# Forgetting attention on one core: one row of 24 score matmuls per head pair, the value products behind it, and two steps issued in another order

## The chip, the cores and the metric

The kernel runs on one core of one Trainium2 chip. The time is the device time of one execution in microseconds (us); three executions were timed, and one more was profiled.

## The reference

A decoder trunk of two layers works on a stream of 512 rows and 1024 columns. The first layer has dilated sliding-window attention and a convolutional feed-forward part; the second, which this case is about, has forgetting attention (16 heads of 64) and a feed-forward part of the same kind. Keys, values and the cumulative log of the forget gates `c` are shared and computed once.

```python
def fox_mixer(xn, w_q, w_o, k, v, c):
    q = (xn @ w_q).reshape(B, T, B_HEADS, HEAD_DIM)
    c_t = c.transpose(0, 2, 1)
    for i in range(T // BLK):                  # four blocks of 128 queries
        q0, q1 = i * BLK, (i + 1) * BLK
        s = jnp.einsum('bqhd,bkhd->bhqk', q[:, q0:q1], k[:, :q1]).astype(jnp.float32) * scale
        s = s + (c_t[:, :, q0:q1, None] - c_t[:, :, None, :q1])
        s = jnp.where(causal, s, NEG)
        p = jax.nn.softmax(s, axis=-1).astype(v.dtype)
        outs.append(jnp.einsum('bhqk,bkhd->bqhd', p, v[:, :q1]))
    o = jnp.concatenate(outs, axis=1)
    return o.reshape(B, T, B_WIDTH) @ w_o
```

## The kernel before

The instructions of every engine are issued in the order in which the program names them. Each engine takes its own in that order and waits where an operand or a buffer is not ready. Products of full precision are made from a high and a low half of each operand, with three matmuls (`mm3`).

The attention stage is a loop over 32 units and three more steps (line 1708). A unit is (j, i): head pair j of 0 to 7, query block i of 0 to 3. A unit passes through several steps, each in a later round of the loop:

- `f_scores` (line 1619): TensorE multiplies queries and keys, 12 matmuls for two blocks of a pair, with two heads side by side in the two 64-row halves of the array. Blocks 0 and 1 share two PSUM banks; blocks 2 and 3 take two banks each. It is called at i = 0 and at i = 2.
- `f_bias` (line 1607): GpSimd makes the forget bias and the causal mask, one unit ahead.
- `f_exp` (line 1633): VectorE adds the bias to the scores and takes the row's maximum in one instruction for each head; ScalarE takes the exponential and its sum.
- `f_norm` (line 1646): VectorE divides the last unit's probabilities by their sums ("scaling").
- `f_transpose` (line 1656): two rounds behind, TensorE turns the probabilities over into PSUM, 2, 4, 6 or 8 blocks of 128 x 128 for i = 0 to 3, and ScalarE copies them out.
- `f_pv` (line 1672): TensorE multiplies them with the values ("value products", 40 matmuls for a pair with a 64-column form of the array). This is done for a whole pair at once, when the loop is at block 2 of the next pair, behind that round's transposes. `f_out_high` (ScalarE) and `f_out_low` (VectorE) then split the output in two halves.

Between these rows TensorE works on the queries of pairs ahead: `q_part(j, i)` (line 1537) is a quarter, six matmuls of 512 columns; `q_high` (ScalarE) and `q_low` (VectorE) split the sum. In the last pairs there are no queries left, and one group of six output-projection matmuls (`po.both`, tile `acc`) a round takes their place.

Weights come in pieces of 512 KB. `W.high` (ScalarE) makes the high half. The low half is made by `W.low` on VectorE (pairs 0, 1 and from 6 on), or, in pairs 2 to 5, by `W.minus` (ScalarE writes the negative of the high half) and `W.low_added` (a DMA issued on GpSimd adds the raw piece). Eight PSUM banks and pools of SBUF buffers are shared; raw pieces, gate rows, biases and probabilities take their buffers from one pool of ten (`p4`).

The lines that set the order of scores, scaling and products:

```python
            if i % 2 == 0:
                f_scores(j, (i, i + 1))
        if 1 <= n <= N:
            f_norm(*units[n - 1])
        if live:
            f_exp(j, i)
        ...
        if n % 4 == 2 or n == N:
            while pv_next < n - 2:
```

Of the kernel before, what the change touches and what calls it, by code (L numbers as in the profile page):

```python
# [117 lines left out]
def trunk_kernel(ctx, tc, x, norm_gains, w_qkv_a, w_o_a, w_q_b, w_o_b, kv_norm, w_kvf, b_f,  # L118
# [11 lines left out]
    def t8(shape, dt=F32, name="t8"):  # L130
        return p8.tile(shape, dt, tag="t8", name=name)

    def t4(shape, dt=F32, name="t4"):
        return p4.tile(shape, dt, tag="t4", name=name)

    def t2(shape, dt=F32, name="t2"):
        return p2.tile(shape, dt, tag="t2", name=name)

    def bank(shape, name="bank"):
        return psp.tile(shape, F32, tag="ps", name=name)  # L140

    def small(n, name):
        return sml.tile([128, n], F32, tag=name, name=name)
# [73 lines left out]
    W = Weights(nc, new_raw, lambda: t8([128, 2, 1024], F32R, name="w"), pieces)  # L217
# [64 lines left out]
    def mm3(o, ah, al, bh, bl, first, last, shared=False):  # L282
        pe.matmul(o, ah, bh, start=first, stop=False, skip_group_check=shared)  # L283
        pe.matmul(o, ah, bl, start=False, stop=False, skip_group_check=shared)  # L284
        pe.matmul(o, al, bh, start=False, stop=last, skip_group_check=shared)  # L285
# [78 lines left out]
    def xs(xT, kc, s):  # L364
        return xT[0][kc // 4][:, kc % 4, s], xT[1][kc // 4][:, kc % 4, s]
# [205 lines left out]
    def down_sums(pairs, place, queue, lag, behind):  # L571


        live, n = [], len(pairs)
        for i in range(n + lag + behind):
            if i < n:
                l, j = pairs[i]
                a, b = place()
                live.append((a, b))
                r = w_down[l][j * 256:j * 256 + 256, :].rearrange("(c p) d -> c p d", p=128)  # L580
                sp.dma_start(a, r[0])
                sp.dma_start(b[:, 0:512], r[1, :, 512:1024])
                sp.dma_start(b[:, 512:1024], r[1, :, 0:512])
            if 0 <= i - lag < n:
                a, b = live[i - lag]
                dve.tensor_tensor(a[:, 0:512], a[:, 512:1024], a[:, 0:512], ALU.subtract)
                dve.tensor_tensor(a[:, 512:1024], b[:, 0:512], a[:, 512:1024], ALU.subtract)
                dve.tensor_tensor(b[:, 0:512], b[:, 0:512], a[:, 0:512], ALU.subtract)
                dve.tensor_tensor(b[:, 512:1024], b[:, 512:1024], b[:, 0:512], ALU.subtract)
            i -= lag + behind  # L590
            if i >= 0:
                l, j = pairs[i]
                for q, t in enumerate(live[i]):
                    queue.dma_start(dT[l][j, :, q * 1024:q * 1024 + 1024], t)
            yield
# [932 lines left out]
    def load_ck(j):  # L1528
        t = t4([128, 2, T], name="ck")
        s = cd[2 * j:2 * j + 2, :]  # L1530
        sp.dma_start(t, bass.AP(tensor=s.tensor, offset=s.offset, ap=[[0, 128], [T, 2], [1, T]]))
        cks[j] = t
# [4 lines left out]
    def q_part(j, i):  # L1537

        if j >= 8:
            return  # L1540
        if i == 0:
            qps[j] = (bank([128, T], name="q_ps"), [t.rearrange("p (k c) -> p k c", k=8) for t in W.get()])
        o, (wh, wl) = qps[j]
        for kc in (2 * i, 2 * i + 1):
            bh, bl = xs(xTq, kc, ALL)
            mm3(o, wh[:, kc, :], wl[:, kc, :], bh, bl, kc == 0, kc == KD - 1)
# [72 lines left out]
    def f_scores(j, blocks):  # L1619
        wide = blocks[0] >= 2  # L1620
        if not wide:
            both = [bank([128, 2, 256], name="s_ps") for _ in range(2)]
        k = kst[j // 2][:, j % 2]
        for i in blocks:
            nn = max(256, (i + 1) * 128)
            sc[j, i] = [bank([128, T], name="s_ps") for _ in range(2)] if wide else [o[:, i] for o in both]
            for qp, kp in ((0, 0), (0, 1), (1, 0)):
                for hh in range(2):
                    own = slice(64 * hh, 64 * hh + 64)
                    pe.matmul(sc[j, i][hh][:, :nn], qT[j][own, qp, i * 128:(i + 1) * 128], k[own, kp, :nn],  # L1630
                              start=qp + kp == 0, stop=qp == 1)

    def f_exp(j, i):
        n = (i + 1) * 128
        s = sc.pop((j, i))
        bias = bia.pop((j, i))
        p = t4([128, 2, T], name="prob")
        nm, ls = small(2, "nm"), small(2, "ls")
        for hh in range(2):
            dve.tensor_tensor_reduce(p[:, hh, :n], s[hh][:, :n], bias[:, hh, :n], -0.125, BIG, ALU.add, ALU.min,  # L1640
                                     nm[:, hh:hh + 1])
            act.activation(p[:, hh, :n], p[:, hh, :n], AF.Exp, bias=nm[:, hh:hh + 1], scale=-1.0,
                           accum_out=ls[:, hh:hh + 1])
        prob[j, i] = (p, ls)

    def f_norm(j, i):
        n = (i + 1) * 128
        p, ls = prob[j, i]
        rl = small(2, "rl")
        dve.reciprocal(rl, ls)  # L1650
        for hh in range(2):
            dve.tensor_scalar(p[:, hh, :n], p[:, hh, :n], rl[:, hh:hh + 1], None, ALU.mult)
# [3 lines left out]
    def f_transpose(j, i):  # L1656
        p, _ = prob.pop((j, i))
        for hh in range(2):
            if i >= 2 or hh == 0:
                o = bank([128, 4, 128], name="pT_ps")  # L1660
                t = t2([128, 4, 128], name="pT")
            k0 = (i + 1) * hh if i < 2 else 0
            for k in range(i + 1):
                pe.transpose(o[:, k0 + k, :], p[:, hh, k * 128:(k + 1) * 128], ident)
            if i >= 2 or hh == 1:
                act.copy(t[:, :k0 + i + 1], o[:, :k0 + i + 1])
            pT[j, i, hh] = t[:, k0:k0 + i + 1]
# [4 lines left out]
    def f_pv(j, i):  # L1672
        if i == 0:
            ops[j] = bank([128, T], name="o_ps")
        o = ops[j]
        for k in range(i + 1):
            for hh in range(2):
                hd = 2 * j + hh
                pe.matmul(o[64 * hh:64 * hh + 64, i * 128:(i + 1) * 128],
                          Vt[hd // 8][:, k, (hd % 8) * 64:(hd % 8) * 64 + 64], pT[j, i, hh][:, k, :],  # L1680
                          start=k == 0, stop=k == i)
        del pT[j, i, 0], pT[j, i, 1]

    def f_out_high(j):
        o = ops[j]
        if j % 2 == 0:
            OTb[j // 2] = t8([128, 2, 2, T], F32R, name=f"OTb{j // 2}")
        t = OTb[j // 2]
        act.copy(t[:, 0, j % 2, :], o)
# [5 lines left out]
    units = [(j, i) for j in range(8) for i in range(4)]  # L1695
# [9 lines left out]
    N = len(units)  # L1705
    pv_next = 0
    down1 = down_sums([(1, 9), (1, 10)], in_one, pool, 2, 0)
    for n in range(N + 3):
        live = n < N
        if live:  # L1710
            j, i = units[n]
            if i == 0 and j + 1 < 8:
                load_ck(j + 1)
            if i % 2 == 0:
                f_scores(j, (i, i + 1))
        if 1 <= n <= N:
            f_norm(*units[n - 1])
        if live:
            f_exp(j, i)
            if n + 1 < N:  # L1720
                f_bias(*units[n + 1])
            if i == 1:
                q_low(j + 1)
                if 2 <= j < 6:
                    W.minus()
                    W.low_added()
            if i == 2 and j < 2 or (j, i) >= (6, 2):
                W.low()
            if i == 3 and j:
                f_out_low(j - 1)  # L1730
            q_part(j + 1 + (i > 0), (i + 3) % 4)
            if (j, i) in ((7, 1), (7, 2)):
                next(down1)
        if 2 <= n < N + 2:
            f_transpose(*units[n - 2])
        if n >= N + 3 - len(fill):
            po.both(*fill[n - N - 3 + len(fill)])

        if n % 4 == 2 or n == N:
            while pv_next < n - 2:  # L1740
                ju, iu = units[pv_next]
                pv_next += 1
                f_pv(ju, iu)
                if iu == 3:
                    f_out_high(ju)
        if live and i == 0:
            q_high(j + 1)
        if live and (i == (j < 2) if j < 6 else (j, i) >= (6, 1) and W.n_split < wo + 4):
            W.high()
# [53 lines left out]
```

## Time and profile before

| | us |
|---|---|
| median of 3 runs | 1109.83 (1109.48 to 1110.65) |
| profiled execution | 1109.52 |
| its span, first to last instruction | 1107.7 |
| TensorE busy | 1098.7 |
| VectorE busy | 876.4 |
| ScalarE busy | 674.2 |
| GpSimd busy | 210.0 |

The span is 1.8 us shorter than the time of the same execution. In the timelines each row has the start and the duration in us, the engine (PE is TensorE's matmuls, PEld its weight loads, DVE VectorE, ACT ScalarE, POOL GpSimd, SP SyncE), the line of the kernel, the operation, the tile written and the tiles read, shapes, and how many such instructions follow one another. In brackets stands how long the engine was idle before it and what ended that. Matmuls overlap, so the distance from start to start tells more than the duration.

### The profile page before, as it was taken

The numbers are of one execution on the slowest core, as the hardware profiler recorded it, in microseconds if no ns is written. First come the engines' busy times: TensorE is split into PE (matmuls) and PEld (weight loads), VectorE is DVE, ScalarE is ACT, GpSimd is POOL, SyncE is SP. The second block draws the span as 40 slices with busy tenths as digits, with TensorE's granted clock in tenths as the row PEclk, the third lists the DMA queues.
The fourth block names the chain that finished last, engine by engine and source line by source line (L and its number), as shares of the span: only waits on it lengthen the run. The fifth ranks groups of instructions, "written<-read, shape, count | busy, mean of one in ns | idle before, by whom it ended". The sixth has DMA issues, their size and how long they took to land.

```text
span 1107.7 us, 18081 instructions
## 1 busy us (share of the span) xinstructions
PE 1098.7 (99%) x6609; PEld 951.8 (86%) x6609; DVE 876.4 (79%) x1493; ACT 674.2 (61%) x1116; POOL 210.0 (19%) x309
## 2 busy tenths in 40 slices
PE   9999999999999999999999999999999999999997
PEld 6988889899999988888888788789999999988886
DVE  6697788888778689997685676868887788779894
ACT  7654565755666656576451587746656666747572
POOL 2532001311111211000001445400411111211000
PEclk9999999999999999999999999999999999999999
DMA  9799854467887979793448435594368878989862
GB/s 324 171 381 412 310 161 134 98 181 190 207 199 185 245 263 328 268 333 103 152 134 301 156 96 127 163 285 121 84 178 208 197 186 189 231 266 324 314 247 76
DMA packets 184928, 236.26 MB, mean 213 GB/s; under 512 B 12352, under 2 KB 132152, under 8 KB 184840
## 3 DMA queue, kind: packets, MB, share of 16 engines
q1 hardware_dynamic: 169224, 182.94, 51.0%
q0 software_dynamic: 14944, 52.18, 20.7%
q8 instruction: 52, 0.85, 0.3%
q14 instruction: 36, 0.29, 0.1%
q10 hardware_dynamic: 672, 0.00, 0.0%
HBM read 166.08 MB, written 39.63 MB: 186 GB/s over the span
## 4 chain that ended last, share of the span: by engine, by line
PE 96%; DVE 1%; ACT 1%; issue 1%; POOL 1%; DMA 0%; DVEq 0%; SPq 0%; POOLq 0%; ACTq 0%
PE up L284 13%; PE up L283 13%; PE up L285 13%; PE acc L283 8%; PE acc L284 8%; PE acc L285 8%; PE v_ps L283 2%; PE v_ps L285 2%; PE v_ps L284 2%; PE qk_ps L284 2%; PE qk_ps L283 2%; PE qk_ps L285 2%; PE q_ps L283 1%; PE first L285 1%; PE first L283 1%; PE first L284 1%
## 5 line engine op out<-in xcount | busy, mean ns | idle before, releaser
L283 PE MATMUL acc<-w 128*128 128x512 f32 (+1 forms) x311 | 120.6, 388 | 0.3 <-DVE mix L332 0.3
L285 PE MATMUL acc<-w 128*128 128x512 f32 (+1 forms) x311 | 120.4, 387 | 0.0
L284 PE MATMUL acc<-w 128*128 128x512 f32 (+1 forms) x267 | 103.2, 387 | 0.0
L78 DVE TENSOR_TENSOR w<-wraw,w 128x1024 fp32r<-128x1024 f32 x62 | 82.3, 1347 | 22.9 <-ACT w L60 22.5
L283 PE MATMUL up<-xsh,w 128*128 128x256 f32 x352 | 99.6, 283 | 0.0
L284 PE MATMUL up<-xsl,w 128*128 128x256 f32 x352 | 99.6, 283 | 0.0
L285 PE MATMUL up<-xsh,w 128*128 128x256 f32 x352 | 99.6, 283 | 0.0
L60 ACT CAST w<-wraw 128x1024 fp32r<-128x1024 f32 x82 | 84.7, 1051 | 18.7 <-PE v_ps L284 6.9
L620 ACT ACTIVATE bb<-up,conv 128x512 f32<-128x512 f32 x80 | 59.8, 778 | 58.3 <-DVE up L1007 47.6
L284 PE MATMUL up<-xcl,w 128*128 128x512 f32 (+1 forms) x276 | 93.5, 339 | 0.0
L284 PE MATMUL up<-xbl,w 128*128 128x512 f32 (+1 forms) x276 | 93.5, 339 | 0.0
L283 PE MATMUL up<-xbh,w 128*128 128x512 f32 (+1 forms) x276 | 93.5, 339 | 0.0
L283 PE MATMUL up<-xch,w 128*128 128x512 f32 (+1 forms) x276 | 93.5, 339 | 0.0
L285 PE MATMUL up<-xbh,w 128*128 128x512 f32 (+1 forms) x276 | 93.4, 338 | 0.0
L285 PE MATMUL up<-xch,w 128*128 128x512 f32 (+1 forms) x276 | 93.4, 338 | 0.0
L283 PEld LDWEIGHTS acc<-w 128*128 128x128 f32 x311 | 58.4, 188 | 12.6 <-DVE mix L332 0.7
L285 PEld LDWEIGHTS acc<-w 128*128 128x128 f32 x311 | 58.4, 188 | 11.9
L283 PEld LDWEIGHTS up<-xsh,w 128*128 128x128 f32 x352 | 67.6, 192 | 0.0
L284 PEld LDWEIGHTS up<-xsl,w 128*128 128x128 f32 x352 | 67.6, 192 | 0.0
L285 PEld LDWEIGHTS up<-xsh,w 128*128 128x128 f32 x352 | 67.6, 192 | 0.0
L621 DVE SCALAR_TENSOR_TENSOR bb<-up,conv,bb 128x511 f32<-128x511 f32 x80 | 59.5, 744 | 6.2 <-ACT bb L620 6.1
L623 DVE SCALAR_TENSOR_TENSOR bb<-up,conv,bb 128x510 f32<-128x510 f32 x80 | 59.9, 749 | 2.8
(312 smaller groups left out, 3151.8 us busy)
## 6 DMA issues: line engine op xcount, KB each, us to landing
wraw<-in_w_up_dram SPq DMA_DIRECT2D x88, 512.0 KB, 5.4
w<-wraw POOLq DMA_DIRECT2D x32, 512.0 KB, 6.4
dT<-dsums SPq DMA_DIRECT2D x28, 512.0 KB, 7.0
w<-wsum POOLq DMA_DIRECT2D x24, 512.0 KB, 5.7
dsums<-in_w_down_dram SPq DMA_DIRECT2D x22, 512.0 KB, 7.6
dsums<-in_w_down_dram SPq DMA_DIRECT2D x44, 256.0 KB, 7.8
hD<-hc POOLq DMA_DIRECT2D x44, 256.0 KB, 6.9
dact<-hD SPq DMA_DIRECT2D x44, 256.0 KB, 5.6
```

What stands on the lines that cost most here:

```text
L60: self.nc.scalar.copy(pair[:, 0], raw)
L78: self.nc.vector.tensor_tensor(pair[:, 1], raw, pair[:, 0].bitcast(F32), ALU.subtract)
L283: pe.matmul(o, ah, bh, start=first, stop=False, skip_group_check=shared)
L284: pe.matmul(o, ah, bl, start=False, stop=False, skip_group_check=shared)
L285: pe.matmul(o, al, bh, start=False, stop=last, skip_group_check=shared)
L620: act.activation(bb[:, s, :], ps, AF.Identity, bias=cp[:, 3, ch:ch + 1], scale=cp[:, 2, ch:ch + 1])
L621: dve.scalar_tensor_tensor(bb[:, s, 1:], ps[:, :T - 1], cp[:, 1, ch:ch + 1], bb[:, s, 1:], ALU.mult, ALU.add)
L623: dve.scalar_tensor_tensor(bb[:, s, 2:], ps[:, :T - 2], cp[:, 0, ch:ch + 1], bb[:, s, 2:], ALU.mult, ALU.add)
```

## The change

The scores of blocks 0 and 1 of the first pair are issued ahead of the loop. At block 2 of each pair the loop issues a query quarter, then the scores of this pair's blocks 2 and 3 and those of the next pair's blocks 0 and 1 as one row of 24, and then the value products of the pair before; the query quarter that this round had further back is left out there. Within a round the maxima and exponentials (`f_exp`) are issued ahead of the last unit's scaling (`f_norm`). `W.minus` and `W.low_added` move behind the round's transposes. In the last rounds the value products stay where they were.

```diff
+    outs = []
+
+    def values_of(n):
+        nonlocal pv_next
+        while pv_next < n - 2:
+            j, i = units[pv_next]
+            pv_next += 1
+            f_pv(j, i)
+            if i == 3:
+                outs.append(j)
+
+    f_scores(0, (0, 1))
     for n in range(N + 3):
         live = n < N
         if live:
             j, i = units[n]
             if i == 0 and j + 1 < 8:
                 load_ck(j + 1)
-            if i % 2 == 0:
-                f_scores(j, (i, i + 1))
+            if i == 2:
+                q_part(j + 2, 1)
+                f_scores(j, (2, 3))
+                if j + 1 < 8:
+                    f_scores(j + 1, (0, 1))
+                values_of(n)
+        if live:
+            f_exp(j, i)
         if 1 <= n <= N:
             f_norm(*units[n - 1])
         if live:
-            f_exp(j, i)
             if n + 1 < N:
                 f_bias(*units[n + 1])
             if i == 1:
                 q_low(j + 1)
-                if 2 <= j < 6:
-                    W.minus()
-                    W.low_added()
...
-            q_part(j + 1 + (i > 0), (i + 3) % 4)
+            if i != 2:
+                q_part(j + 1 + (i > 0), (i + 3) % 4)
...
             f_transpose(*units[n - 2])
+        if live and i == 1 and 2 <= j < 6:
+            W.minus()
+            W.low_added()
...
-        if n % 4 == 2 or n == N:
-            while pv_next < n - 2:
-                ju, iu = units[pv_next]
-                pv_next += 1
-                f_pv(ju, iu)
-                if iu == 3:
-                    f_out_high(ju)
+        if n >= N and n % 4 in (0, 2):
+            values_of(n)
+        while outs:
+            f_out_high(outs.pop())
```

## The prediction

> **What bounds the kernel now.** I read the page first, then the busy time of the attention stage by windows, then TensorE's timeline there, and last the timelines of the engines that feed it.
>
> ```profile
> PE 1098.7 (99%) x6609; PEld 951.8 (86%) x6609; DVE 876.4 (79%) x1493; ACT 674.2 (61%) x1116; POOL 210.0 (19%) x309
> ```
>
> TensorE is busy for 99% of the span, so only TensorE time counts, and its busy time also hides waits, because the ends of matmuls are modelled. The stage that the change touches runs from about 620 us, the first score matmul, to about 728 us. One head pair in the middle of it, by windows (columns: PE, PEld, DVE, ACT, POOL busy):
>
> ```profile
> 655.50:668.50 13.00, 13.00 (x110) 10.54 (x109) 8.58 (x30) 10.16 (x27) 6.95 (x13) 1.00 0.51 114
> ```
>
> TensorE fills the 13 us; VectorE has 4.4 us spare, ScalarE 2.8, and the granted clock is 1.00. TensorE's timeline of the same pair (start, us, operation), where the distance between starts is the cost:
>
> ```profile
> 655.96 0.98 PE L1630 MATMUL s_ps<-kst,qst 64*128 64x256 f32 x12
> 656.87 0.50 PE L283 MATMUL q_ps<-xqh,w 128*128 128x512 f32 x1
> ...
> 658.36 0.82 PE L1664 MATMUL pT_ps<-ident,prob 128*128 128x128 f32 x6
> 658.94 0.48 PE L283 MATMUL q_ps<-xqh,w 128*128 128x512 f32 x1
> ...
> 660.40 1.03 PE L1664 MATMUL pT_ps<-ident,prob 128*128 128x128 f32 x8
> 661.37 1.49 PE L1630 MATMUL s_ps<-kst,qst 64*128 64x384 f32 x12
> 662.78 0.50 PE L283 MATMUL q_ps<-xqh,w 128*128 128x512 f32 x1
> ...
> 664.28 0.38 PE L1664 MATMUL pT_ps<-ident,prob 128*128 128x128 f32 x2
> 664.59 2.40 PE L1679 MATMUL o_ps<-pT,Vt 128*64 128x128 f32 x40
> 666.92 0.50 PE L283 MATMUL q_ps<-xqh,w 128*128 128x512 f32 x1
> ...
> 668.95 0.98 PE L1630 MATMUL s_ps<-kst,qst 64*128 64x256 f32 x12
> ```
>
> A period is 668.95 - 655.96 = 12.99 us: two score rows of 0.91 and 1.41, four groups of six query matmuls, transposes in rows of 6, 8, 2 and 4, and 40 value products of 2.33. Nothing waits, but the price of a row depends on what follows it. Here are the other neighbours, and the places where TensorE does wait:
>
> ```profile
> 627.43 0.38 PE L1664 MATMUL pT_ps<-ident,prob 128*128 128x128 f32 x2
> 627.57 0.48 PE L283 MATMUL q_ps<-xqh,w 128*128 128x512 f32 x1
> ...
> 634.99 1.87 PE L1630 MATMUL s_ps<-kst,qst 64*128 64x384 f32 x12
> 636.79 0.50 PE L283 MATMUL q_ps<-xqh,w 128*128 128x512 f32 x1
> ...
> 703.08 0.66 PE L1664 MATMUL pT_ps<-ident,prob 128*128 128x128 f32 x4
> 703.49 0.48 PE L283 MATMUL acc<-w,OTb 128*128 128x512 f32 x1
> ...
> 708.62 1.17 PE L1664 MATMUL pT_ps<-ident,prob 128*128 128x128 f32 x8 [0.41 <-DVE prob L1652]
> ...
> 710.77 0.39 PE L285 MATMUL acc<-w,OTb 128*128 128x512 f32 x1
> 711.09 2.01 PE L1630 MATMUL s_ps<-kst,qst 64*128 64x384 f32 x12
> 713.39 0.44 PE L1664 MATMUL pT_ps<-ident,prob 128*128 128x128 f32 x2 [0.30 <-ACT pT L1666]
> ...
> 722.32 1.09 PE L1664 MATMUL pT_ps<-ident,prob 128*128 128x128 f32 x8
> 723.17 0.48 PE L283 MATMUL acc<-w,OTb 128*128 128x512 f32 x1
> ```
>
> Two transposes cost 0.14 ahead of query matmuls (627.43), but 0.31 ahead of value products (664.28). Eight cost 0.85 ahead of ordinary matmuls (722.32), but 0.97 ahead of scores (660.40). Four cost 0.41 even right behind value products (703.08). An ordinary matmul ahead of scores takes 0.32 (710.77) against the usual 0.23. Waits: the score row at 634.99 takes 1.80 where 661.37 takes 1.41, so 0.4 is lost; at 708.62 0.57 is lost (the last product ahead started 0.81 earlier and needs 0.23); at 711.09 the row takes 2.0 instead of 1.41 and 0.3 more follow. That is 0.4 in the first pair and 1.5 in the last two.
>
> **The change, part by part.**
>
> *Score rows of 24, value products behind.* Nothing is added or removed; rows are moved. Per pair TensorE now runs: six query matmuls ahead of scores (660.40 - 658.94 = 1.46, plus 0.09 for the switch, 1.55), 24 scores (1.41 + 0.91 = 2.32), a switch x, 40 products (2.33), two transposes ahead of query matmuls (0.14), six matmuls (1.46), four transposes (0.41), 1.46, six transposes (0.58), 1.46, eight transposes (0.85). The sum is 12.56 + x. The price x of going from scores straight to products is not in the trace. From below it is about 0, which is what two transposes ahead of query matmuls show; from above 0.17, the difference of 0.31 and 0.14 that products cost behind transposes. I take 0.08, in between, because both neighbours are array-form changes, and neither is nearer. A period is then 12.64, which saves 0.35.
>
> The Trainium skill, TensorEngine Tiling (Array Packing), Overview, says that a change of tiling mode drains TensorE. The 0.09 to 0.17 per switch above agree, and by that rule alone x would be a full switch at 0.17, a period 12.73, and the gain 0.6 us smaller over seven rows.
>
> The four periods between the first and fifth row of products save 4 x 0.35 = 1.4. In front of the first row of products the same terms save 0.4, and the 0.4 wait goes, because the second pair's query is split several rows ahead of its scores: 0.8.
>
> *What feeds the moved rows.* The scores of the next pair's blocks 0 and 1 now come two units earlier. Their query low half (q_low) is issued one unit ahead on VectorE. Counting a period from the query matmuls ahead of the score row, q_low ends at about 12.2 us and its scores start at 12.6 + 2.9 = 15.5: cover 3.3. Banks: 6 for scores, 1 for the query sum, 1 for the products make all 8; the last two come from the transposes of the pair before, copied by about 1.8, needed at 2.9 and 3.9: cover 1.1, which costs its lack if gone. The copy of (j,0) and the high half of the output (f_out_high) now stand behind the products on ScalarE, with exp(j,3) queued behind both:
>
> ```profile
> 667.04 0.59 ACT L1689 CAST OTb<-o_ps 128x512 fp32r<-128x512 f32 x1 [1.43 <-PE o_ps L1679]
> 667.52 0.73 ACT L1642 ACTIVATE prob<-prob,nm 128x512 f32<-128x512 f32 x1
> ```
>
> ScalarE already waits 1.43 there for the products, and exp(j,3) already stands behind that. Now: products end at 6.3, transposes 6.4, copy until 6.9, output 7.4 (0.48 from start to start, 667.04 to 667.52), exp of two heads 1.43 until 8.8, scaling of the first head 9.7. Its transposes are due at 12.64 - 0.85 = 11.8: cover 2.1. Cost nothing.
>
> *Minus of weight pieces later* (pairs 2 to 5). GpSimd's row behind the weight DMA, and the landing of that DMA in this stage (512 KB each, us) and in the whole kernel:
>
> ```profile
> 655.79 0.94 POOL L1612 TENSOR_SCALAR bias<-ck,cq 128x256 f32<-128x256 f32 x2 [1.28 <-DMA w<-wraw]
> ```
>
> ```profile
> w<-wraw POOLq DMA_DIRECT2D x4, 512.0 KB, 5.5
> ```
>
> ```profile
> w<-wraw POOLq DMA_DIRECT2D x32, 512.0 KB, 6.4
> ```
>
>  ScalarE copies the transposes of (j-1,3) first (two copies, 0.95), then does the minus. The products, now due earlier, gain that; the DMA that adds the piece is issued about 1 us later on GpSimd, and bias(j,3) is queued behind it. Minus ends at about 2.8, issue 0.7, bias 2.1: 5.6. The maximum of (j,3) then runs from 5.6 to 6.8, its exp was to start at 7.4 anyway. Cover 1.1; SyncE's queue is passed by nothing, and the query group that moves ahead of the scores issues no DMA (only a pair's first group takes a weight). The piece is used a pair later, so its 5.5 us landing is covered.
>
> *Maxima ahead of scaling.* VectorE's work is the same; exp starts earlier by one scaling (0.5 to 1.2), scaling later by one maximum (0.4 to 1.2), against 2 us of cover. Nothing in the middle of the stage.
>
> *The last two pairs.* Query matmuls are gone, output products fill in one group a unit. Rows: the 34.9 us from the fifth row of products to the end of the loop (692.9 to 727.8) include one score row of 0.91 that is now done earlier, so 34.0 stand against 32.0 of the new order without waits. Does it wait? VectorE's queue: the first late weight's high half ends on ScalarE at 699.9 (new time), then its low half 1.2, maximum (6,3) 1.2, scaling (6,2) 1.1, second low half 1.2, output low 0.6, maximum (7,0) 0.4, first head's scaling (6,3) 0.8: 706.5. TensorE reaches the transposes of (6,3) at 705.5. The low half is the longest of these terms on VectorE, a row of before:
>
> ```profile
> 702.19 1.23 DVE L78 TENSOR_TENSOR w<-wraw,w 128x1024 fp32r<-128x1024 f32 x1
> ```
>
> So one wait of 1.0 remains in place of 1.5, for 33.0: saved 1.0.
>
> Sum: 0.8 + 1.4 + 1.0 = 3.2, call it 3.1. Behind the stage TensorE waits for no engine for more than 0.4 us at once, so the gain is kept. The profiled execution took 1109.52, the median of the runs is 1109.83, 0.31 above it; against the profiled one the forecast is 1106.4, against the median 1106.7, the number that I give. x at 0 or 0.17 moves it by 0.6 either way, the last wait at 0 or 2 us by 1.0; both are seldom at one end, so I take 2.0 to 4.2 saved.
>
> **Rivals.**
>
> *The switches are worth little and the waits only move.* x is 0.17 and the last pairs lose 1.5 to 2 as before, since VectorE's queue there holds the same instructions. For it: 708.62 already waits for a scaling, and my own re-adding leaves 1.0. Saved: 0.4 + 0.4 + 4 x 0.26 + 0.3, less about 0.4 for longer waits: 1.7, to 1108.1. That is within 0.2% (2.2 us), about what a measurement of this kernel can tell from no change.
>
> *A buffer loop through the weight DMA makes it slower.* The pool of ten 4-KB-row buffers holds raw weights, biases and probabilities alike, and 655.79 shows a bias waiting for the weight DMA, since it took the piece's buffer. With the release now behind that of a probability tile, the next owner changes. If it is the probability tile of (j,3), its maximum waits for the landing, and a ring closes: issue and landing 5.6, half a maximum 0.7, then on ScalarE exp 1.43, copy 0.48, exp 0.8, copies 0.75, q_high 0.48, weight high 0.96, exp 1.0, copies 0.95, minus 0.95: 14.1 us. It decides when the ring exceeds TensorE's 12.64, so when the landing takes over 4.0; at 5.5 it adds 1.5 per pair in four pairs, at the 6.4 of all such DMAs on the page 2.4. Less the 2 us of cover that is the 3.9 to 7.4 us lost: 0.8 to 4.3 slower, 1112.3 in the middle. Against it: before, the owner was a tile six allocations later, which has 1.7 us of cover in the new order too.
>
> The Trainium skill, PSUM — Partial Sum Buffer, Engine vs sequencer instructions, says that the queues of ScalarE, VectorE and GpSimd are strictly first in, first out; the trace agrees (bias behind the DMA issue, exp behind the output copy), and the ring needs just that.
>
> **How the numbers follow.** The forecast gets 0.55, the moved waits 0.28, the buffer ring 0.17. Nearly all of the forecast is over 2.2 us: faster 0.53. Within 0.2%: 0.28, 0.02 of the forecast and the 0.04 of the ring that ends below 2.2 us: 0.34. Slower: 0.13. The low end is 1105.3, a little under the 4.2 saved; the high end 1110.9 takes in the moved waits and the cheap end of the ring.
>
> **What would show it.** Right: one row of 24 scores and 40 products back to back in 4.6 to 4.8 us, periods of about 12.6, no wait at the second pair's scores, about 1 us of wait at (6,3), and the convolution transposes at about 724.7 instead of 727.8. The switch is mis-sized if the first product starts over 0.2 behind the scores' 2.32. Wrong: maxima of block 3 that wait for the weight DMA, periods over 13 in pairs 2 to 5, or score rows that wait for banks.

## The result, and the profile after

The changed kernel took 1108.04 us in the median of 18 runs (1106.91 to 1109.94), the kernel before 1109.78 (1109.38 to 1110.81) beside it: a ratio of 0.9983, interval 0.9976 to 0.9990. The same kernel run twice more, with the experiments, took 1107.16 and 1107.28, which is 2.7 and 2.8 us under the kernel before. Its profiled execution took 1107.3, with a span of 1105.5, against 1109.52 and 1107.7.

The engine rows of the page after:

```profile
PE 1095.3 (99%) x6609; PEld 951.4 (86%) x6609; DVE 878.3 (79%) x1493; ACT 672.3 (61%) x1116; POOL 213.3 (19%) x309
```

Nothing is added or removed, and TensorE's busy time falls by 3.4 us. Here is one head pair in the middle, from one row of products to the next, by windows (PE, PEld, DVE, ACT, POOL busy):

```profile
676.48:688.84 12.36, 12.36 (x111) 10.51 (x109) 9.77 (x31) 10.00 (x28) 7.57 (x14) 1.00 0.48 129
```

The period is 12.36 where it was 12.99. TensorE's timeline of that period (start, us, operation):

```profile
672.78 0.47 PE L283 MATMUL q_ps<-xqh,w 128*128 128x512 f32 x1
...
674.34 2.21 PE L1630 MATMUL s_ps<-kst,qst 64*128 64x384 f32 x24
676.48 2.40 PE L1679 MATMUL o_ps<-pT,Vt 128*64 128x128 f32 x40
678.82 0.44 PE L1664 MATMUL pT_ps<-ident,prob 128*128 128x128 f32 x2
679.01 0.48 PE L283 MATMUL q_ps<-xqh,w 128*128 128x512 f32 x1
...
680.49 0.60 PE L1664 MATMUL pT_ps<-ident,prob 128*128 128x128 f32 x4
680.84 0.47 PE L283 MATMUL q_ps<-xqh,w 128*128 128x512 f32 x1
```

The row of 24 scores takes 676.48 - 674.34 = 2.14 and the products 2.34, with no wait between. At both ends of the stage TensorE does wait:

```profile
632.36 0.55 PE L1664 MATMUL pT_ps<-ident,prob 128*128 128x128 f32 x3 [0.17 <-DVE prob L1652]
633.11 0.52 PE L1664 MATMUL pT_ps<-ident,prob 128*128 128x128 f32 x3 [0.21 <-DVE prob L1652]
...
694.69 2.14 PE L1664 MATMUL pT_ps<-ident,prob 128*128 128x128 f32 x14
696.76 2.62 PE L1630 MATMUL s_ps<-kst,qst 64*128 64x384 f32 x24
699.31 2.40 PE L1679 MATMUL o_ps<-pT,Vt 128*64 128x128 f32 x40
...
705.56 0.40 PE L285 MATMUL acc<-w,OTb 128*128 128x512 f32 x1
707.03 0.66 PE L1664 MATMUL pT_ps<-ident,prob 128*128 128x128 f32 x4 [1.07 <-DVE prob L1652]
707.96 0.63 PE L1664 MATMUL pT_ps<-ident,prob 128*128 128x128 f32 x4 [0.27 <-ACT pT L1666]
...
725.54 0.44 PE L566 MATMUL cv_ps<-ident,cv_rows 44*128 44x44 f32 x4
```

The stage, from the first score matmul to the transposes of the convolution, runs from 621.18 to 725.54: 104.36 us, where it took 107.15 (620.63 to 727.78). That is 2.8 less, and it comes from the middle: between the first and fifth row of products 51.97 became 49.51, 2.46 less. The first pair and the last two gave 0.3 together.

The waits between the pairs' products (three periods, 651 to 690), in the view of waits (engine, line, tile, released by: us, times, longest), first of the kernel before, then of the kernel after:

```profile
DVE rl L1650 <- ACT prob L1642: 12.3, 12, 1.3
```

```profile
DVE prob L1640 <- PE s_ps L1630: 9.1, 4, 2.7
```

Before, VectorE stood at each scaling (`rl`) until ScalarE had the exponentials of the same unit, 4 us in each pair. After, that wait is gone, and VectorE waits for TensorE's scores instead. The experiments e5 and e6 come back to this line.

### The profile page after: what moved, and what is told of

The parts are those of the page before. It is cut to its first block, busy times and chain, and to the rows that moved or that the text cites. A ratio compares the mean times of both kernels' runs of the same rounds, so it can differ in the third digit from the quotient of the medians.

```text
span 1105.5 us, 18058 instructions
## 1 busy us (share of the span) xinstructions
PE 1095.3 (99%) x6609; PEld 951.4 (86%) x6609; DVE 878.3 (79%) x1493; ACT 672.3 (61%) x1116; POOL 213.3 (19%) x309
## 4 chain that ended last, share of the span: by engine, by line
PE 94%; ACT 2%; DVE 1%; DMA 1%; issue 1%; POOL 0%; SPq 0%; DVEq 0%; ACTq 0%; POOLq 0%
PE up L284 13%; PE up L283 13%; PE up L285 13%; PE acc L283 9%; PE acc L285 8%; PE acc L284 8%; PE v_ps L283 2%; PE v_ps L285 2%; PE v_ps L284 2%; PE qk_ps L284 2%; PE qk_ps L283 2%; PE qk_ps L285 2%; PE first L285 1%; PE first L283 1%; PE first L284 1%; PE k_ps L285 1%
## 5 line engine op out<-in xcount | busy, mean ns | idle before, releaser
L283 PEld LDWEIGHTS acc<-w 128*128 128x128 f32 x311 | 58.4, 188 | 12.4 <-DVE mix L332 0.7
```

## Experiments

All profiles share the marks used above. The period is that of the pairs between the first and fifth row of products; the stage goes from the first score to the convolution's transposes. The medians stand beside 1109.86 us of the kernel before for e1 to e4, 1109.77 for e5 and e7 to e9, and 1110.06 for e6, e10 and e11.

| kernel | period | stage | median | ratio, 95% interval |
|---|---|---|---|---|
| before | 12.99 | 107.15 | | |
| after | 12.35 to 12.40 | 104.36 | 1108.04 | 0.9983, 0.9976 to 0.9990 |
| e1 rows only | 12.92 to 12.97 | 106.88 | 1109.65 | 0.9999, 0.9990 to 1.0008 |
| e2 swap only | 12.99 | 105.98 | 1109.74 | 0.9998, 0.9989 to 1.0006 |
| e3 late minus only | 12.98 to 14.26 | 109.79 | 1112.31 | 1.0021, 1.0012 to 1.0030 |
| e4 after again | 12.35 to 12.40 | 104.13 | 1107.16 | 0.9977, 0.9968 to 0.9987 |
| e5 rows and swap | 12.35 to 12.40 | 104.11 | 1106.89 | 0.9976, 0.9966 to 0.9986 |
| e6 rows, late minus | 12.38 to 12.97 | 107.16 | 1109.90 | 0.9998, 0.9989 to 1.0007 |
| e7 low halves on VectorE | 12.35 to 12.40 | 103.87 | 1107.64 | 0.9980, 0.9971 to 0.9989 |
| e8 add later | 12.39 to 13.04 | 104.72 | 1107.17 | 0.9975, 0.9965 to 0.9985 |
| e9 rows of 12 | 12.76 to 13.28 | 106.07 | 1107.70 | 0.9983, 0.9975 to 0.9992 |
| e10 order at the end | 12.35 to 12.40 | 103.30 | 1106.11 | 0.9965, 0.9952 to 0.9977 |
| e11 after, third time | 12.35 to 12.40 | 104.07 | 1107.28 | 0.9975, 0.9966 to 0.9984 |

### The three parts alone (e1, e2, e3)

e1: the rows of 24 with the products behind them, with scaling first and the minus early as before.

```diff
 (against the kernel after)
-        if live:
-            f_exp(j, i)
         if 1 <= n <= N:
             f_norm(*units[n - 1])
         if live:
+            f_exp(j, i)
...
+                if 2 <= j < 6:
+                    W.minus()
+                    W.low_added()
```

> The rows of 24 with the value products behind, but minus where it was and scaling ahead of the maxima as before. Theory (the saving is TensorE's switches between array forms): periods of about 12.4 us stay, the stage keeps about 2.3 to 2.8 us of saving, the median lies 1.5 to 2.8 us below the kernel before, within 0.6 us of the changed kernel. Rival (the saving needs the maxima early and the minus late, since the rows alone make transposes wait): TensorE waits appear in pairs 2 to 5, periods of 12.7 or more, less than 1 us below before.

The rows alone bring nothing: period 12.96, ratio 0.9999. TensorE's timeline of e1:

```profile
674.11 1.61 PE L1630 MATMUL s_ps<-kst,qst 64*128 64x384 f32 x13
675.96 0.98 PE L1630 MATMUL s_ps<-kst,qst 64*128 64x256 f32 x11 [0.23 <-ACT pT L1666]
676.87 2.40 PE L1679 MATMUL o_ps<-pT,Vt 128*64 128x128 f32 x40
```

and ScalarE's beside it:

```profile
674.39 1.06 ACT L71 ACTIVATE w<-wraw 128x1024 fp32r<-128x1024 f32 x1
675.34 1.06 ACT L1666 COPY pT<-pT_ps 128x512 f32<-128x512 f32 x2
```

The row of 24 takes 2.76 in place of 2.14, since the banks for the next pair's scores wait for the copies of the transposes, and those stand behind the minus (L71). From this alone the late minus seems to be what the rows need. e5 and e6 show that it isn't.

e2: only the maxima ahead of the scaling.

```diff
+        if live:
+            f_exp(j, i)
         if 1 <= n <= N:
             f_norm(*units[n - 1])
         if live:
-            f_exp(j, i)
```

> The kernel before with the maxima and exponentials issued ahead of the last unit's scaling, nothing else. Theory: periods stay 12.99 us, since TensorE waits for nothing in the middle; only the waits of the last two pairs can move, so within 0.8 us of before, with a longer wait at the transposes of (6,3), whose scaling comes later. Rival: the early maxima carry a good part of the saving, 1 us or more below before.

The periods stay at 12.99, but the stage is 1.17 shorter: 0.38 in front of the first row of products, 0.77 behind the sixth. The median does not show it (1109.74, with runs from 1108.41 to 1111.78).

e3: only the minus and the adding DMA behind the transposes.

```diff
-                if 2 <= j < 6:
-                    W.minus()
-                    W.low_added()
...
             f_transpose(*units[n - 2])
+        if live and i == 1 and 2 <= j < 6:
+            W.minus()
+            W.low_added()
```

> The kernel before with minus and the adding DMA behind the round's transposes, nothing else. Theory: nothing on TensorE changes, periods 12.99 us, within 0.4 us of before; the bias of block 3 starts about 1 us later behind the DMA issue on GpSimd. Rival (a buffer ring through the weight DMA): maxima of block 3 wait for the landing and periods of pairs 2 to 5 grow to 13.2 us or more, 1 us or more above before.

2.45 us slower. GpSimd's timeline of e3, and the landing of the adding DMA in the window 640 to 695:

```profile
678.92 0.88 POOL L98 DMA_DIRECT2D w<-wraw  x1 [2.19 <-ACT w L71]
...
687.38 0.94 POOL L1612 TENSOR_SCALAR bias<-ck,cq 128x256 f32<-128x256 f32 x2 [4.41 <-DMA w<-wraw]
```

```profile
w<-wraw POOLq DMA_DIRECT2D x4, 512.0 KB, 7.9
```

The bias waits for the landing in all four pairs, and the landing takes 7.9 where it took 5.5 (the median of four each). The issue now comes 0.1 to 0.3 us ahead of the load of the gate rows `ck`, where it came 1.2 to 1.3 ahead in the kernel before; that this is what makes the landing longer was not tested by itself. TensorE loses the time where it reads the piece:

```profile
673.65 0.50 PE L285 MATMUL q_ps<-xqh,w 128*128 128x512 f32 x1 [0.91 <-DMA w<-wraw]
```

By start-to-start distances that group of six query matmuls takes 2.65 and the one a period later 2.06, in place of 1.47. Landing, bias, maximum, exponentials, copies, minus and the next issue follow one another, 14.37 from issue to issue (664.55 to 678.92). It is the buffer ring of the prediction in kind, but it runs over a bias and not over a probability tile, and of the combinations run here it closes in this one alone. In the kernel after the same rows read

```profile
676.30 0.88 POOL L98 DMA_DIRECT2D w<-wraw  x1 [3.94 <-ACT w L71]
...
680.52 1.25 POOL L1612 TENSOR_SCALAR bias<-ck,cq 128x256 f32<-128x256 f32 x2 [0.25 <-DVE rl L1650]
```

```profile
w<-wraw POOLq DMA_DIRECT2D x4, 512.0 KB, 5.1
```

and no bias waits for the DMA there.

### Which of the two small moves the rows need (e5, e6)

e5: rows and early maxima, the minus early as before (the kernel after with the second piece of e1's diff). e6: rows and late minus, scaling first (the kernel after with the first piece of e1's diff).

> The changed kernel with minus and the adding DMA back ahead of the round's transposes. Theory (late minus gives back the PSUM banks in time): the scores of the next pair wait again for ScalarE's copies of the transposes, by 0.5 to 0.7 us in each of pairs 2 to 5, periods of about 12.9 to 13.0 there, 1.5 to 2.5 us above the changed kernel. Rival (the early maxima give the time in the last pairs and the ramp, minus is nothing): periods of 12.4, within 0.6 us of the changed kernel.

> The kernel after with scaling ahead of maxima again: rows of 24 and late minus, without the early maxima. Open is which of the two small moves gives the rows their gain: rows alone kept a period of 12.96, rows with early maxima alone 12.39. Theory: what the score row needs is that ScalarE's copies of the last unit's transposes stand ahead of the minus; with the minus late they do, so either of the two moves is enough. Middle periods 12.4, no wait of the score row for copies; the ramp and the last pairs are about 1 us worse than in the kernel after (the early maxima alone saved 1.17 in the stage), so a stage of 105.0 to 105.5 against 104.35. Rival: it is the early exponentials that free ScalarE for the copies; then the late minus does not help, the period stays at 12.9 as with rows alone and the stage at 106.5 to 107. Second rival: with scaling first the buffer ring through the weight DMA that late minus alone closed (biases waiting 3 to 5 us for it) comes back: periods over 13 and a stage over 108.

e5 has the whole gain, period 12.35 to 12.40; e6 has none, its periods go 12.38, 12.64, 12.97, 12.95. So "the late minus frees the copies" fell, and the early exponentials hold. The reason begins on ScalarE's timeline. In e5 the minus is still ahead of the copies:

```profile
673.84 0.53 ACT L1642 ACTIVATE prob<-prob,nm 128x256 f32<-128x256 f32 x1
...
674.84 1.06 ACT L71 ACTIVATE w<-wraw 128x1024 fp32r<-128x1024 f32 x1
675.78 1.07 ACT L1666 COPY pT<-pT_ps 128x512 f32<-128x512 f32 x2
```

Its score row starts at 675.55 (products at 677.69, less 2.14), so the exponentials of that unit begin 1.7 us ahead of the row, and the copies 0.2 behind its start, in time. In e6:

```profile
673.80 1.62 PE L1630 MATMUL s_ps<-kst,qst 64*128 64x384 f32 x13
675.62 0.96 PE L1630 MATMUL s_ps<-kst,qst 64*128 64x256 f32 x11 [0.21 <-ACT pT L1666]
```

```profile
673.99 0.52 ACT L1642 ACTIVATE prob<-prob,nm 128x256 f32<-128x256 f32 x1
...
674.99 1.07 ACT L1666 COPY pT<-pT_ps 128x512 f32<-128x512 f32 x2
```

The minus is out of the way, but the exponentials begin 0.2 behind the row's start, so the copies come 1.2 behind it, as late as in e1. The view of waits leads to the cause: e1 and e6 keep the wait of the kernel before, e5 has lost it (0.6 in the same three periods).

```profile
DVE rl L1650 <- ACT prob L1642: 12.0, 12, 1.3
```

```profile
DVE rl L1650 <- ACT prob L1642: 10.9, 12, 1.3
```

With scaling first, VectorE's scaling of a unit waits for ScalarE's exponentials of it, the next maxima stand behind that scaling, and the next exponentials wait for those maxima. In e1 this is one link of a ring that also goes through TensorE. Here are its rows one period ahead of those above, on TensorE, on ScalarE and on VectorE:

```profile
662.99 0.98 PE L1630 MATMUL s_ps<-kst,qst 64*128 64x256 f32 x11 [0.17 <-ACT pT L1666]
```

```profile
666.76 0.37 ACT L1666 COPY pT<-pT_ps 128x256 f32<-128x256 f32 x1 [2.13 <-PE pT_ps L1664]
...
667.51 0.74 ACT L1642 ACTIVATE prob<-prob,nm 128x512 f32<-128x512 f32 x1
...
670.45 0.40 ACT L1642 ACTIVATE prob<-prob,nm 128x128 f32<-128x128 f32 x1 [0.93 <-ACT pT L1666]
```

```profile
669.07 0.17 DVE L1650 RECIPROCAL rl<-ls 128x2 f32<-128x2 f32 x1 [0.72 <-ACT prob L1642]
...
670.07 0.29 DVE L1640 CUSTOM_DVE_ANT_0 prob<-s_ps,bias 128x128 f32<-128x128 f32 x1
```

A copy frees a bank, and the score row goes on at 662.99. Then come the second half of the score row, the products and two transposes on TensorE; the copy (666.76), the output copy and the exponentials of (j,3) on ScalarE (667.51); their scaling (669.07) and the next unit's maximum (670.07) on VectorE; the next exponentials (670.45) and, behind them in ScalarE's queue, copies, two high halves, two more exponentials, the minus (674.39) and the copies (675.34) that free the bank again at 675.96. That is 12.97 around, the period of e1. (The view puts the wait of 0.93 down to ScalarE's own copy ahead, but that had ended at 669.5; the maximum was out at 670.37.)

In e6 the minus is out of that ring, but a second one closes without TensorE, between VectorE and ScalarE, with GpSimd beside it:

```profile
678.43 1.86 DVE L1652 TENSOR_SCALAR prob<-prob,rl 128x384 f32<-128x384 f32 x2
```

```profile
677.93 1.67 POOL L1612 TENSOR_SCALAR bias<-ck,cq 128x512 f32<-128x512 f32 x2
```

```profile
680.93 0.72 ACT L1642 ACTIVATE prob<-prob,nm 128x512 f32<-128x512 f32 x1 [0.75 <-DVE nm L1640]
...
684.00 0.40 ACT L1642 ACTIVATE prob<-prob,nm 128x128 f32<-128x128 f32 x1 [1.07 <-DVE nm L1640]
```

From the copies at 674.99 it goes over the minus, the exponentials and the scaling of (j,2) (678.43), the maximum and exponentials of (j,3) (680.93), their scaling and the next unit's maximum and exponentials (684.00) to the next copies at 687.93: 12.94, the period of e6. The scaling of 384 columns takes 1.86 here, while GpSimd makes a bias; in e1 it took 0.92 (from 664.87), most of it behind that bias, which ended at 665.09.

Both rings hold ScalarE's wait for the next unit's maximum, 0.93 and 1.07 us in each pair, and the early maxima take it out of both: in e5 that exponential (670.79) follows the copy ahead of it without a wait, and TensorE's own 12.37 is the longest again. In the kernel before neither ring is the limit. TensorE waits for nothing in its middle, and the exponentials of (j,3) start 0.4 behind their maximum there (667.52 against 667.11), because ScalarE stands waiting for the products; so breaking the link alone (e2) leaves TensorE's 12.99. That both rings come out within 0.05 of the old period has no common reason that a run shows.

### What a row's company costs (e9)

e9: the kernel after with the next pair's 12 scores on their own again, as in the kernel before.

```diff
+            if i == 0 and j:
+                f_scores(j, (0, 1))
             if i == 2:
                 q_part(j + 2, 1)
                 f_scores(j, (2, 3))
-                if j + 1 < 8:
-                    f_scores(j + 1, (0, 1))
                 values_of(n)
```

> The changed kernel with two score rows of 12 per pair: blocks 2 and 3 ahead of the value products as now, blocks 0 and 1 two rounds later on their own as before. Theory (a row of 24 saves the switches and the drain between): a period costs 0.3 to 0.45 us more than 12.37, 1.2 to 2.5 us above the changed kernel. Rival (the rows' length is nothing, the place of the products is all): periods of 12.4 to 12.5 us.

```profile
675.18 1.50 PE L1630 MATMUL s_ps<-kst,qst 64*128 64x384 f32 x12
676.62 2.40 PE L1679 MATMUL o_ps<-pT,Vt 128*64 128x128 f32 x40
...
680.63 0.60 PE L1664 MATMUL pT_ps<-ident,prob 128*128 128x128 f32 x4
681.16 0.98 PE L1630 MATMUL s_ps<-kst,qst 64*128 64x256 f32 x12
682.07 0.50 PE L283 MATMUL q_ps<-xqh,w 128*128 128x512 f32 x1
```

Twelve scores ahead of products take 1.44, as many ahead of query matmuls took 1.41. The other twelve take 0.91 alone and 2.14 - 1.44 = 0.70 inside the row of 24, and four transposes ahead of them 0.53 instead of 0.35. 0.21 + 0.18 = 0.39, and the period is 0.39 longer (12.76 against 12.37). The fourth period, 13.28, has eight transposes that take 1.12 instead of 0.79, which is a lack of its own at the end and was left aside.

### The adding DMA (e7, e8)

e7 makes the low halves on VectorE in all pairs, without the minus and the DMA; e8 issues the minus a unit later.

```diff
 (e7)
-            if i == 2 and j < 2 or (j, i) >= (6, 2):
+            if i == 2 and j < 6 or (j, i) >= (6, 2):
                 W.low()
...
-        if live and i == 1 and 2 <= j < 6:
-            W.minus()
-            W.low_added()
 (e8)
+            if i == 2 and 2 <= j < 6:
+                W.minus()
+                W.low_added()
...
-        if live and i == 1 and 2 <= j < 6:
-            W.minus()
-            W.low_added()
```

> The changed kernel with the low halves of the weight pieces of pairs 2 to 5 made by VectorE, as in pairs 0 and 1, so without minus and without the adding DMA. Theory on the spread (some executions wait for the landing of the adding DMA ahead of the third query matmul): periods stay 12.4 us, the spread over the executions shrinks to under 1.2 us, median 1106.6 to 1107.4. Rival (the 1.2 us more on VectorE per pair cost more than the DMA): transposes wait for the scaling, periods of 12.8 or more, 1 us or more above the changed kernel. Rival on the spread (it lies outside the stage): it stays 2 us or more.

> The changed kernel with minus and the adding DMA one step later still, behind the exponentials and the bias of block 3, so that the DMA is issued about 2 us later. Theory (the cover of the landing is about 2 us): TensorE now waits for the weight DMA at query matmuls of pairs 3 to 6 in most executions, 0.5 to 2 us in sum, more in some, median 0.5 to 2.5 us above the changed kernel and a spread of 2 us or more. Rival (the piece is needed a whole pair later and the landing is covered): within 0.4 us of the changed kernel, or below it since block 3's bias no longer stands behind the DMA issue.

e7 keeps the periods of 12.4: VectorE has room there for four more low halves of 1.2. e8 shows how much slack the landing has. One query matmul waits for it, and that period takes 13.04:

```profile
PE q_ps L285 <- DMA w<-wraw: 0.4, 1, 0.4
```

Two us of delay use the cover up, but the median stays. Neither kernel explains why single executions of the kernel after differ by up to 3 us: e7 has no such DMA and still spans 1106.88 to 1108.52.

### The kernel after, again, and a better order at the end (e4, e11, e10)

> The changed kernel once more, word for word, for the spread of its times (1106.9 to 1109.9 over 18 executions, against 1109.4 to 1110.8 of before). Theory: the attention stage takes 104.4 us in every execution, and what varies lies outside it, in places where TensorE waits for a DMA. Rival: the stage itself varies, by 1 us or more, because a wait behind the weight DMA opens in some executions.

> The kernel after, word for word, beside the other two on the same chip. The stage from the first score to the transposes of the convolution should take 104.1 to 104.4 again, and 379.98 us should follow it. If the spread of the times lies outside the stage, the profile's start of the stage differs from the 621.18 and 621.43 of the two profiles so far, or what follows does, while the stage stays within 0.3; if it lies in the stage, the stage differs by as much as the span does. Time 1107 to 1108.

The stage took 104.36, 104.13 and 104.07 in the three profiles, and from its end to the last instruction 380.0 each time. Other profiles show what else moves: in e5 the stage begins at 622.37, where the kernel after has 621.18, and 380.8 us follow it, though its stage is as short (104.11). In these profiles what varies lies mostly outside the stage, in code that the change doesn't touch; what makes it was not found.

e10: e5 with two steps on VectorE in another order in the last two pairs.

```diff
-        if live:
+        if live and n != 28:
             f_exp(j, i)
         if 1 <= n <= N:
             f_norm(*units[n - 1])
         if live:
+            if n == 28:
+                f_exp(j, i)
...
-            if i == 2 and j < 2 or (j, i) >= (6, 2):
-                W.low()
             if i == 3 and j:
                 f_out_low(j - 1)
+            if i == 2 and j < 2 or (j, i) >= (6, 2):
+                W.low()
```

> Rows of 24 and early maxima, minus early as before, and two moves on VectorE in the last pairs: at unit (6,3) the low half of the output ahead of the low half of the weight, and at unit (7,0) the scaling of (6,3) ahead of the maximum of (7,0), so that the transposes of (6,3) don't wait for about 1.6 us of other VectorE work. Theory: the wait of 1.1 to 1.3 us there is only an order on VectorE; it falls to 0.3 or less and nothing later in the stage takes its place, so the stage is about 1 us shorter than the 104.1 of rows and early maxima: 103.1. Rival: TensorE arrives earlier at the next row that needs VectorE or ScalarE (scores of blocks 2 and 3 of the last pair, or the transposes of (7,0) and (7,1)) and waits there instead: stage 103.8 to 104.3, no gain.

```profile
705.54 0.66 PE L1664 MATMUL pT_ps<-ident,prob 128*128 128x128 f32 x4 [0.51 <-DVE prob L1652]
706.36 0.63 PE L1664 MATMUL pT_ps<-ident,prob 128*128 128x128 f32 x4 [0.16 <-DVE prob L1652]
```

The wait at (6,3) is halved rather than gone (0.67 against 1.34), nothing later takes its place, and the stage is 103.30. At 1106.11 us (five runs, 1105.72 to 1106.40) it is the fastest kernel here, 3.95 us under the kernel before and 1.2 under the kernel after on the same chip.

## Why the prediction was right, and where it was not

The forecast was 1106.7, with 3.1 us saved. The stage gave 2.8, 3.0 and 3.1 in three profiles of the kernel after, the medians 1.7, 2.7 and 2.8. The stage is the right one and the size is near; the split within the stage is not right, since the middle gave more than forecast and the ends gave less. That the errors cancel is luck.

**The periods: 0.35 forecast, 0.62 found.** The step that failed is the row price. The prediction took 1.41 + 0.91 from rows that each ended in a change of array form, and then added x = 0.08 for one more. e9 shows that products behind scores cost 0.03 more than query matmuls do, so x was counted twice, and that the change between the two rows of scores is gone from the merged row (0.21): 2.14 in place of 2.40. No other term is off by more than 0.06, and together they cancel. Four periods gave 2.46, not 1.4. The sign that the prediction named, 24 scores and 40 products in 4.6 to 4.8, came out at 4.48. The Trainium skill, TensorEngine Tiling (Array Packing), Tiling Modes, Key Properties, says that TensorE drains where the tiling mode changes. The trace agrees: 0.21 goes with the change that is taken out, and the change from scores to products lies within the 1.44, as the one to query matmuls lies within the 1.41. The 12.73 that the prediction worked out from the rule counted that change a second time.

**The first pair and the last two: 1.8 forecast, 0.3 to 0.6 found.** From the first score to the first row of products 17.96 went by before (620.63 to 638.59) and 18.15 after (621.18 to 639.33), but a score row of 0.91 now lies ahead of that row and two transposes of 0.31 behind it. With these set right, the first pair gave 17.96 + 0.91 - 0.31 - 18.15 = 0.4 of its 0.8, and the last two next to nothing of their 1.0 (34.9 - 0.91 + 0.31 = 34.3 before, 34.4 after, 34.1 in the two repeats). In the first pair the wait at the second pair's scores went, but a wait of 0.17 + 0.21 at the transposes of (0,2) came, 0.8 by start-to-start distances, for scalings that now stand behind the next maxima; the prediction had only the middle of the stage in view for that move. In the last two the forecast allowed one wait of 1.0 beside 32.0 of work. That wait is there, 1.07 and 0.27, and it costs 1.6 by start-to-start distances. With it come a row of 14 transposes of 2.07, where e10's takes 1.62 (694.34 to 695.96), and a row of 24 scores of 2.55 instead of 2.14. From the fifth row's products to the end 34.4 went by instead of 33.0; the step that failed here is that nothing but that one wait would be lost.

**Maxima ahead of scaling: "nothing in the middle of the stage".** This is the step whose reasoning was wrong though its number did no harm. By windows VectorE had 4.4 us to spare and ScalarE 2.8, and the prediction read that as slack. But once the rows are moved, the link from exponentials over scaling to the next maxima lies in rings of 12.97 and 12.94 (e1, e6), longer than TensorE's 12.37. Without this move the rows would have gained nothing (e1, e6).

**Minus later: cost nothing, with cover.** Right in the kernel after. Beside the early maxima it brings nothing (e5 and the three profiles of the kernel after differ by at most 0.25 in the stage), beside the rows alone nothing either (e6), and by itself it costs 2.45 (e3). The cover for the banks, 1.1 in the forecast, was smaller: the two copies take ScalarE from 673.98 to 675.05, and the next pair's scores follow at about 675.75 (674.34 and the 1.41 of twelve scores), 0.7 later. The landing was not covered by "a pair": e8 uses its cover up with 2 us of delay, and in e3 TensorE waits for the piece.

**The rivals.** "The switches are worth little and the waits only move" holds for the ends of the stage and fails for the middle. Its time, 1108.1, is that of the first measurement (1108.04), and nearer to it than the forecast's 1106.7; it is the stage, and the repeats at 1107.16 and 1107.28, that speak against it. The buffer ring exists, but it is cheaper than it was priced: its loss was put at 3.9 to 7.4 before the gain was taken off, and e3, which has no such gain, lost 2.45. In the kernel after it stays open: 680.52 above follows without a wait for the DMA.

## What to carry to other kernels

Engines that each show spare time can be the limit together, when their waits close a ring: before counting idle time as slack, follow who ends whose wait until the path comes back, and add up its length. A change that gains nothing alone may be the one that lets another gain, so undo parts one at a time and in pairs. Price a row of matmuls by its start-to-start distance with the neighbour that it will have, and don't count the change of array form both in the row and beside it.

## What the runs showed of the hardware

The 512 KB adding DMA landed in 5.1 us (after), 5.5 (before) and 7.9 (e3; 6.9 to 9.1 in its four), where it was issued 0.1 to 0.3 us ahead of the load of the gate rows. Twelve score matmuls cost 0.91 us as a row of their own and 0.70 behind others of the same form. Twelve scores cost 1.44 with value products right behind them and 1.41 with query matmuls behind them. Two scalings of 384 columns on VectorE took 0.92 in e1 and 1.86 in e6, where GpSimd made a bias at the same time.
